# Weight buffers at alternating 64-byte offsets, and the later adaLN columns ordered behind a low part on VectorE, in a two-layer hybrid decoder trunk

## The chip, the cores and the metric

The kernel runs on one core of one Trainium2 chip, in one launch. The metric is the device time of that core in microseconds. Three runs of the kernel before gave 904.12, 908.38 and 950.62 us, with the median at 908.38 us. The execution that the profiler took, on which every row below rests, took 906.63 us; its span from the first to the last instruction is 904.9 us, so 1.7 us lie around the span.

## The reference, cut to what matters

Two layers work on x of 256 positions by 1024 features in float32. Each layer computes

```python
mod = c_act @ ada_w + ada_b                     # 1024 -> 3 x 1024: shift, scale, gate
h = rmsnorm(x, norm_g) * (1 + scale) + shift
z = h @ w_in                                    # 1024 -> 13312, for all three branches
ya = rg_lru(causal_dwconv(a_x)) * silu(a_g)     # branch A
yb = merged dilated window attention * silu(b_g)  # branch B: 3 groups x 8 heads x 64
yc = rmsnorm(gla_chunked(c_q, c_k, c_v)) * silu(c_g)  # branch C: 4 heads
merged = mg0 * (ya @ proj_a) + mg1 * (yb @ proj_b) + mg2 * (yc @ proj_c)
x = x + gate * (merged @ w_o)
```

The adaLN product `c_act @ ada_w` has one row only. The kernel treats it as 24 columns of 128 outputs a layer: shift and scale are the first 16 columns, the gate is the last 8.

## The kernel before, in words

All weights come from memory in a fixed stream of 288 units, 144 a layer (`layer_units`, line 39). The order in a layer is: q, k, v and b_g of the first head pair; then the head pairs and branch A mixed; mA (units 68 to 75) and pA (76 to 83), with the attention of the last head pair beside them; c0 to c3 (units 84 to 107); mC, pC, mB, pB and wo (units 108 to 143). In the second layer every number is 144 higher. There are two kinds of unit for what follows:

- **F and P units** (and b_g): the weight is the stationary operand, loaded 128 columns at a time, and 256 positions of the activations move past it. `mm_f` (lines 803 to 809) issues three matmuls for each of 8 slices of the contraction: high weight by high activation, high by low, low by high.
- **Streamed units** (kind "T" other than b_g): 128 positions of the activations are stationary and 384, 400 or 512 weight columns move (`mm_t`, lines 775 to 801), again three matmuls for each slice.

Each weight is split in two for float32r: ScalarE casts the loaded tile `raw` to the high part `whi` (line 232), and VectorE subtracts to get the low part `wlo` (line 233). `advance(i + 3)` does this for the unit three ahead of the one TensorE works on, so there are four buffers of `whi` and four of `wlo`, and six of `raw`. A buffer has 1040 floats, that is 4160 bytes, 64 more than a multiple of 256, so that buffers which lie one behind the other start 64 bytes further past a multiple of 256 each time. The kernel then lets a unit use the buffer from its start or from 64 bytes in (`o`, line 225). In the built program the four buffers of the high parts lie together, and those of the low parts lie together. With `o`, the weights of the units i = 0, 1, 2, 3 (modulo 4) start 64, 192, 192, 64 bytes past a multiple of 256 in F and P units, high and low alike, and 0, 0, 128, 128 in streamed units. The activations start at 0 (`hhi`, `hlo`, `mhi`, `mlo`) or at 128 (`yhi`, `ylo`).

The adaLN columns run in the same stream. A column is a 512 KB transfer into a `raw` buffer on SyncE's queue (line 208) and one custom reduction of 128x1024 on VectorE (`ada_tile`, line 334), with a small read of its accumulator behind it; every second one has a product of one column behind it (line 336). Sixteen columns of the first layer run at the start, ahead of the units they belong to (`START`). The other 32 stand one behind every third unit, from unit 68 of each layer on (`REST`): the first layer's gate and the second layer's shift and scale (24 columns, units 68 to 137), and in the second layer its gate (8 columns, units 212 to 233).

The program is written in this order, but a scheduler orders each engine's instructions by its own estimate of when they can start, unless `tc.issue_after` holds one behind another. Nothing holds the 32 later columns in the kernel before. Each engine then works strictly in its order: while VectorE waits for a column's transfer, the low parts and the evacuations behind it wait too.

Of the kernel before, what the change touches and what calls it, by code (L numbers as in the profile page):

```python
# [10 lines left out]
F32 = mybir.dt.float32  # L11
F32R = mybir.dt.float32r
I32 = mybir.dt.int32
AF = mybir.ActivationFunctionType
ALU = mybir.AluOpType
# [3 lines left out]
D, S, L, P = 1024, 256, 2, 128  # L19
# [53 lines left out]
def unit_elems(u):  # L73
    return {"T": 2 * u[4], "F": 1024, "P": 1024}[u[0]]
# [52 lines left out]
def hybrid_trunk(ctx: ExitStack, tc: tile.TileContext, ws, ada, vec, gates, a2, qkg, c_t, x_t, pos, inv, eye,  # L127
                 mask, tri, rst, out):
    nc = tc.nc
    V, A, G, T, SY = nc.vector, nc.scalar, nc.gpsimd, nc.tensor, nc.sync  # L130
# [10 lines left out]
    wts = ctx.enter_context(tc.tile_pool(name="wts", bufs=LEAD + 1))  # L141
# [42 lines left out]
    cur = {}  # L184


    raw_t, w_t = {}, {}
    at_item = [0, 0]
    early = {}

    def load_next():
        n = at_item[0]
        if n >= len(items):
            return
        at_item[0] += 1
        it = items[n]
        if it in early:
            raw_t[n] = early[it]
            cur["sy", "a", it[2]] = SY.dma_start(out=early[it], in_=ada[it[1], it[2]]).ins
            return load_next()  # L200
        if it[0] == "u":
            e = unit_elems(units[it[1]][1])
            o = offs[it[1]]
            t = wts.tile([P, e], F32, name="raw", tag="raw", bufs=NRAW)
            cur["sy", it[1]] = SY.dma_start(out=t, in_=ws[o:o + e * P].rearrange("(p n) -> p n", p=P)).ins
        else:
            t = wts.tile([P, D], F32, name="raw", tag="raw", bufs=NRAW)
            SY.dma_start(out=t, in_=ada[it[1], it[2]])
        raw_t[n] = t

    def advance(i):

        while at_item[1] < len(items):
            n = at_item[1]
            it = items[n]
            if it[0] == "u" and it[1] > i:
                return
            at_item[1] += 1
            r = raw_t.pop(n)
            if it[0] == "u":  # L220
                e = unit_elems(units[it[1]][1])


                streamed = units[it[1]][1][0] == "T" and units[it[1]][1][1] != "bg"
                o = 16 * ((it[1] % 2 == 0) != streamed)
                hi = wts.tile([P, D + 16], F32R, name="whi", tag="whi")[:, o:o + e]
                lo = wts.tile([P, D + 16], F32R, name="wlo", tag="wlo")[:, o:o + e]
                with ExitStack() as st:
                    if it[1] < 4:
                        st.enter_context(tc.issue_after(cur["ra"]))  # L230
                        st.enter_context(tc.issue_after(cur["rv"]))
                    A.copy(hi, r)  # L232
                    V.tensor_tensor(lo, r, hi.bitcast(F32), ALU.subtract)  # L233
                w_t[it[1]] = (hi, lo)
            else:
                ada_tile(it[1], it[2], r)
            load_next()


# [64 lines left out]
    def vcol(l, c, n=1):  # L304
        return vec_sb[:, l, c:c + n]
# [24 lines left out]
    def ada_tile(l, c, w):  # L330
        a, b = acc[:, l, c:c + 1], vec_sb[:, l, V_ADA + c:V_ADA + c + 1]
        j, i = (c // 2, c % 2) if c < 16 else (c - 16, 2)
        m = mod[:, l, i, j:j + 1]
        V.tensor_tensor_reduce(w, w, crow2, 1.0, b, ALU.mult, ALU.add, a if i == 0 else m)  # L334
        if i == 0:
            V.tensor_tensor(m, a, vcol(l, V_NG + j), ALU.mult)
        if l == 0 and i == 1:
            h_tile(0, j, cur["rstd"], cur["h"])
# [24 lines left out]
    def h_tile(l, j, rstd, h):  # L363
        hi, lo = h
        t = tmp()
        V.scalar_tensor_tensor(t, x_sb[:, j], mod[:, l, 0, j:j + 1], rstd, ALU.mult, ALU.mult)
        sh = mod[:, l, 1, j:j + 1]
        a = A.activation(hi[:, j], t, AF.Identity, bias=sh)  # L368
        v = V.scalar_tensor_tensor(lo[:, j], t, sh, hi[:, j].bitcast(F32), ALU.add, ALU.subtract)  # L369
        cur["h_last"] = (a.ins, v.ins)  # L370
# [443 lines left out]
    def layer(l, h, first_extra):  # L814
# [6 lines left out]
        for i in range(base, base + per_layer):  # L821
            kind, nm, p, kk, n = units[i][1]
            advance(4 * (i // 4) + 3 if i < 12 else i + LEAD)
            if i in first_extra:
                first_extra[i]()
# [255 lines left out]
```

## Time and profile before

| what | value |
|---|---|
| median of three runs | 908.38 us |
| profiled execution | 906.63 us, span 904.9 us |
| TensorE (PE) busy | 865.6 us, 96% |
| VectorE (DVE) busy | 671.9 us, 74% |
| ScalarE (ACT) busy | 531.8 us, 59% |
| GpSimd (POOL) busy | 179.1 us, 20% |
| mean granted TensorE clock | 0.987 of full speed |
| DMA | 170.16 MB, mean 188 GB/s |

The busy share of TensorE says that it has something in flight nearly always. Matmuls overlap in the records, so the time that one takes off the next is read from the starts of two that follow each other, not from the duration of one. The list of costly groups gives the number of matmuls of each kind; the list of waits says for whom an engine sat idle; and the table of windows compares stretches. A good comparison is inside this kernel: both layers do the same work from unit 68 on, except that 24 adaLN columns run there in the first layer and 8 in the second.

### The profile page before, as it was taken

To read this page: it belongs to the slowest core of one execution; us is meant where nothing else is said; L and a number is where in the kernel's file an instruction comes from. 1 tells how busy PE (TensorE), PEld (TensorE's weight loads), DVE (VectorE), ACT (ScalarE), POOL (GpSimd) and SP (SyncE) were. 2 spreads that over 40 slices of the span, in tenths; PEclk is the share of its full clock that TensorE was granted. 3 is DMA by queue.
4 is the path that set the end of the run, shared out by engine and by line. 5 is a ranking of instruction groups with operands and counts; after the bars stand their busy time and mean duration, and the time that the engine had idled before them with its cause. 6 is when DMAs were issued, how large, how long until landed. Compare 5 with 4: busy or idle time off the path is not lost.

```text
span 904.9 us, 16407 instructions
## 1 busy us (share of the span) xinstructions
PE 865.6 (96%) x6340; PEld 818.7 (90%) x6340; DVE 671.9 (74%) x1115; ACT 531.8 (59%) x897; POOL 179.1 (20%) x160
## 2 busy tenths in 40 slices
PE   3989999999999999999999999989999999999998
PEld 2978999999988888998989999979999988899998
DVE  6998899669667667656776788986896666656674
ACT  4376976686544554644454689666874545554451
POOL 0026365224000110100030525651430001000000
PEclk7999999999999999999999999999999999999999
DMA  8884456446756666676654644553567455455651
GB/s 334 309 290 138 146 174 193 141 134 195 248 184 197 205 212 201 212 236 205 224 168 148 191 146 144 176 194 117 184 205 239 163 189 166 148 173 187 191 167 47
DMA packets 52111, 170.16 MB, mean 188 GB/s; under 512 B 6240, under 2 KB 8160, under 8 KB 52032
## 3 DMA queue, kind: packets, MB, share of 16 engines
q1 hardware_dynamic: 51216, 167.04, 56.8%
q10 hardware_dynamic: 672, 1.87, 0.7%
q8 instruction: 50, 0.82, 0.4%
q0 software_dynamic: 144, 0.20, 0.2%
q14 instruction: 29, 0.24, 0.1%
HBM read 168.23 MB, written 1.05 MB: 187 GB/s over the span
## 4 chain that ended last, share of the span: by engine, by line
PE 51%; DVE 19%; DMA 12%; issue 8%; ACT 5%; POOL 4%; DVEq 0%; SPq 0%; ACTq 0%
DMA raw<-in_ada_dram 10%; PE mm L807 10%; PE mm L809 10%; PE mm L808 10%; DVE wlo L233 8%; PE mm L799 5%; PE mm L800 5%; PE mm L801 4%; POOL ss L570 2%; PE xps L177 1%; ACT whi L232 1%; DVE raw L334 1%; DVE rb L564 1%; DMA g_raw<-in_gates_dram 1%; DVE ra L562 1%
## 5 line engine op out<-in xcount | busy, mean ns | idle before, releaser
L233 DVE TENSOR_TENSOR wlo<-raw,whi 128x1024 fp32r<-128x1024 f32 (+2 forms) x288 | 335.3, 1171 | 84.5 <-ACT whi L232 83.1
L232 ACT CAST whi<-raw 128x1024 fp32r<-128x1024 f32 (+2 forms) x288 | 280.1, 976 | 185.2 <-PE mm L808 120.4
L807 PE MATMUL mm<-hhi,whi 128*128 128x256 f32 x768 | 217.1, 283 | 2.9 <-DVE rb L564 2.9
L809 PE MATMUL mm<-hhi,wlo 128*128 128x256 f32 x768 | 216.0, 282 | 3.5 <-DVE wlo L233 3.5
L808 PE MATMUL mm<-hlo,whi 128*128 128x256 f32 x768 | 215.4, 280 | 0.0
L799 PE MATMUL mm<-whi,hhi 128*128 128x384 f32 (+2 forms) x480 | 169.5, 358 | 7.2 <-ACT hhi L368 6.5
L800 PE MATMUL mm<-wlo,hhi 128*128 128x384 f32 (+2 forms) x480 | 171.3, 358 | 1.6 <-DVE wlo L233 1.4
L801 PE MATMUL mm<-whi,hlo 128*128 128x384 f32 (+2 forms) x480 | 167.6, 355 | 0.5 <-DVE hlo L369 0.5
L807 PEld LDWEIGHTS mm<-hhi,whi 128*128 128x128 f32 x768 | 146.0, 190 | 4.5 <-ACT tmp L857 2.9
L809 PEld LDWEIGHTS mm<-hhi,wlo 128*128 128x128 f32 x768 | 145.6, 190 | 4.7 <-DVE wlo L233 4.1
L808 PEld LDWEIGHTS mm<-hlo,whi 128*128 128x128 f32 x768 | 145.7, 190 | 0.3
L799 PEld LDWEIGHTS mm<-whi,hhi 128*128 128x128 f32 x480 | 92.9, 195 | 14.5 <-ACT hhi L368 7.5
L800 PEld LDWEIGHTS mm<-wlo,hhi 128*128 128x128 f32 x480 | 93.4, 195 | 9.1 <-DVE wlo L233 3.2
L334 DVE CUSTOM_DVE_ANT_0 raw<-raw,crow,vec_sb 128x1024 f32<-128x1024 f32 x38 | 48.7, 1283 | 70.2 <-DMA raw<-in_ada_dram 70.2
L801 PEld LDWEIGHTS mm<-whi,hlo 128*128 128x128 f32 x480 | 92.5, 194 | 6.7 <-DVE hlo L369 0.8
L807 PE MATMUL mm<-yhi,whi 128*128 128x256 f32 x320 | 89.9, 281 | 1.5 <-DVE mg L949 1.5
L808 PE MATMUL mm<-ylo,whi 128*128 128x256 f32 x320 | 89.4, 279 | 0.0
L809 PE MATMUL mm<-yhi,wlo 128*128 128x256 f32 x320 | 89.2, 279 | 0.0
L807 PEld LDWEIGHTS mm<-yhi,whi 128*128 128x128 f32 x320 | 60.4, 189 | 2.5 <-DVE mg L949 1.7
L809 PEld LDWEIGHTS mm<-yhi,wlo 128*128 128x128 f32 x320 | 60.1, 188 | 0.8 <-DVE mod L334 0.4
L808 PEld LDWEIGHTS mm<-ylo,whi 128*128 128x128 f32 x320 | 60.1, 188 | 0.0
L708 POOL TENSOR_TENSOR at_hl<-att_sb,at_hl 128x384 fp32r<-128x384 f32 x8 | 8.8, 1096 | 206.3 <-ACT at_hl L707 206.3
(236 smaller groups left out, 1409.2 us busy)
## 6 DMA issues: line engine op xcount, KB each, us to landing
raw<-in_ws_dram SPq DMA_DIRECT2D x192, 512.0 KB, 4.2
raw<-in_ws_dram SPq DMA_DIRECT2D x88, 384.0 KB, 3.1
raw<-in_ada_dram SPq DMA_DIRECT2D x38, 512.0 KB, 4.5
raw<-in_ws_dram SPq DMA_DIRECT2D x8, 400.0 KB, 4.6
g_raw<-in_gates_dram ACTq DMA_DIRECT2D x3, 512.0 KB, 4.5
x_sb<-in_x_t_dram SPq DMA_DIRECT2D x2, 512.0 KB, 6.6
ada_yhi<-in_ada_dram SPq DMA_DIRECT2D x2, 512.0 KB, 7.8
ada_ylo<-in_ada_dram SPq DMA_DIRECT2D x2, 512.0 KB, 9.0
```

The lines of the kernel that those rows point to most:

```text
L177: seen[0] = T.transpose(*a, **k).ins
L232: A.copy(hi, r)
L233: V.tensor_tensor(lo, r, hi.bitcast(F32), ALU.subtract)
L334: V.tensor_tensor_reduce(w, w, crow2, 1.0, b, ALU.mult, ALU.add, a if i == 0 else m)
L562: V.tensor_tensor(ra.rearrange("p (g s) d -> p g s d", g=3), z4, ctab[l][:, i, t].unsqueeze(2).to_broadcast(bc), ALU.mult)
L570: G.tensor_tensor(ss, ss, mhalf[:, 0:12].rearrange("p (a b) -> p a b", a=2), ALU.pow)
L799: T.matmul(o, ah, wh, start=(k == 0), stop=False)
L800: T.matmul(o, ah, wl, start=False, stop=False)
L801: T.matmul(o, al, wh, start=False, stop=(k == KT - 1))
L807: T.matmul(ps[:, 0:S], hi[:, a:b], xh[:, k], start=(k == 0), stop=False)
L808: T.matmul(ps[:, 0:S], hi[:, a:b], xl[:, k], start=False, stop=False)
L809: T.matmul(ps[:, 0:S], lo[:, a:b], xh[:, k], start=False, stop=(k == nk - 1))
```

## The change

Two things change in `advance`. The buffers get a tag each (`whi0` to `whi3`, `wlo0` to `wlo3`, one buffer a tag), in place of four under one tag, and the offset no longer depends on whether the unit is even. In the built program the buffers now lie in turn, a high one, a low one, a high one. With the new offsets the weights of an F or P unit start 64 bytes past a multiple of 256 when the unit's number is even and 192 when it is odd, high and low alike. In a streamed unit the high part starts at 0 and the low part at 128 when the unit's number is even, and the other way round when it is odd. And each of the 32 later columns is held behind the low part that was issued last before it in the program; the first 16 are left as they were.

```diff
     raw_t, w_t = {}, {}
+    early_cols = {(0, c) for c in range(16)}
     at_item = [0, 0]
...
                 streamed = units[it[1]][1][0] == "T" and units[it[1]][1][1] != "bg"
-                o = 16 * ((it[1] % 2 == 0) != streamed)
-                hi = wts.tile([P, D + 16], F32R, name="whi", tag="whi")[:, o:o + e]
-                lo = wts.tile([P, D + 16], F32R, name="wlo", tag="wlo")[:, o:o + e]
+                o, q = 16 * streamed, it[1] % 4
+                hi = wts.tile([P, D + 16], F32R, name="whi", tag=f"whi{q}", bufs=1)[:, 16 - o:16 - o + e]
+                lo = wts.tile([P, D + 16], F32R, name="wlo", tag=f"wlo{q}", bufs=1)[:, o:o + e]
...
-                    V.tensor_tensor(lo, r, hi.bitcast(F32), ALU.subtract)
+                    cur["lo"] = V.tensor_tensor(lo, r, hi.bitcast(F32), ALU.subtract).ins
                 w_t[it[1]] = (hi, lo)
+            elif it[1:] in early_cols:
+                ada_tile(it[1], it[2], r)
             else:
-                ada_tile(it[1], it[2], r)
+
+                with tc.issue_after(cur["lo"]):
+                    ada_tile(it[1], it[2], r)
             load_next()
```

Counted by low parts, the first of the 32 columns stood behind the low part of unit 64 on VectorE and now stands behind that of unit 68; those for units 125, 128, 131, 134 and 137 stood behind 121, 124, 127, 130 and 133. All now stand behind exactly the low part that the program writes ahead of them, three to five low parts later than before. GpSimd and SyncE keep their order; on TensorE a piece of attention or of branch C moves by a unit at some places.

VectorE around unit 124 of the first layer, where mB begins, before (L233 is the low part, L334 the column and its accumulator read, L336 the column's product, L642 the last part of the attention, L921 and L922 pC's evacuation):

```order
L233 TENSOR_TENSOR wlo<-raw,whi 128x1024
L921 SCALAR_TENSOR_TENSOR mg<-mg,mm 128x256
L922 TENSOR_TENSOR mrg<-mrg,mg 128x256
L233 TENSOR_TENSOR wlo<-raw,whi 128x1024
L642 SCALAR_TENSOR_TENSOR ylo<-sgb,yhi 128x1024
L334 ISA raw,mod<-raw,crow,vec_sb 128x1024
L334 ISA mod 128x1
L233 TENSOR_TENSOR wlo<-raw,whi 128x1024 x3
L334 ISA raw,acc<-raw,crow,vec_sb 128x1024
L334 ISA acc 128x1
L233 TENSOR_TENSOR wlo<-raw,whi 128x1024
```

The same place in the changed program, whose line numbers are 2 higher for the low part and 6 higher for the rest:

```order
L927 SCALAR_TENSOR_TENSOR mg<-mg,mm 128x256
L928 TENSOR_TENSOR mrg<-mrg,mg 128x256
L235 TENSOR_TENSOR wlo<-raw,whi 128x1024
L648 SCALAR_TENSOR_TENSOR ylo<-sgb,yhi 128x1024
L235 TENSOR_TENSOR wlo<-raw,whi 128x1024
L340 ISA raw,acc<-raw,crow,vec_sb 128x1024
L340 ISA acc 128x1
L342 TENSOR_TENSOR mod<-acc,vec_sb 128x1
L235 TENSOR_TENSOR wlo<-raw,whi 128x1024 x3
L340 ISA raw,mod<-raw,crow,vec_sb 128x1024
L340 ISA mod 128x1
```

The column that stood between the attention's last part and three low parts now has one of these low parts ahead of it, and it is the column of an earlier place in the stream. The other place is the attention of the last head pair, beside pA. Before (L608 and L611 are the softmax, L634 its result, L915 pA's evacuation):

```order
L634 TENSOR_TENSOR sgb<-xps,sgb 128x2x128
L915 SCALAR_TENSOR_TENSOR mrg<-mg,mm 128x256
L334 ISA raw,mod<-raw,crow,vec_sb 128x1024
L334 ISA mod 128x1
L233 TENSOR_TENSOR wlo<-raw,whi 128x1024
L608 ISA pr,st<-ps_s,m_sb 128x512
L608 ISA st 128x1
L608 ISA pr,st<-ps_s,m_sb 128x512
L608 ISA st 128x1
L611 RECIPROCAL st<-st 128x1
```

In the changed program:

```order
L614 ISA pr,st<-ps_s,m_sb 128x512
L614 ISA st 128x1
L614 ISA pr,st<-ps_s,m_sb 128x512
L614 ISA st 128x1
L617 RECIPROCAL st<-st 128x1
L921 SCALAR_TENSOR_TENSOR mrg<-mg,mm 128x256
L617 RECIPROCAL st<-st 128x1
L235 TENSOR_TENSOR wlo<-raw,whi 128x1024
L340 ISA raw,mod<-raw,crow,vec_sb 128x1024
L340 ISA mod 128x1
L921 SCALAR_TENSOR_TENSOR mrg<-mg,mm 128x256
```

The column that stood ahead of this softmax now stands behind it and behind a low part.

## Rows read from the trace of the kernel before

**Rows 1.** Waits of VectorE, whole span: engine line waited for, us in total, times, longest.

```profile
DVE wlo L233 <- ACT whi L232: 83.1, 84, 2.1
DVE raw L334 <- DMA raw<-in_ada_dram: 70.2, 28, 4.7
```

**Rows 2.** The same waits, first layer from unit 68 on.

```profile
DVE raw L334 <- DMA raw<-in_ada_dram: 59.9, 21, 4.7
```

**Rows 3.** Windows: window, us, PE PEld DVE ACT POOL busy (x), PEclk, DMA share, GB/s.

```profile
276.90:359.70 82.80, 81.28 (x514) 70.25 (x512) 58.80 (x115) 42.37 (x75) 6.20 (x9) 1.00 0.66 214
720.10:800.10 80.00, 80.00 (x512) 69.72 (x512) 51.35 (x92) 43.39 (x78) 7.37 (x10) 1.00 0.53 172
406.40:432.90 26.50, 24.34 (x195) 23.93 (x194) 17.55 (x24) 11.34 (x16) 0.00 (x0) 0.94 0.68 216
846.00:868.10 22.10, 22.10 (x194) 22.10 (x193) 11.79 (x11) 11.33 (x16) 0.00 (x0) 1.00 0.63 191
432.90:468.30 35.40, 33.77 (x290) 33.22 (x289) 27.54 (x46) 18.48 (x29) 8.14 (x6) 1.00 0.65 202
868.10:901.40 33.30, 33.30 (x290) 33.25 (x288) 21.67 (x40) 12.35 (x18) 0.00 (x0) 1.00 0.29 93
420.60:424.00 3.40, 3.40 (x16) 3.40 (x17) 2.11 (x2) 0.00 (x0) 0.00 (x0) 0.50 1.00 290
```

**Rows 4.** Timeline of VectorE around mB: start us, us, instruction [idle before <-releaser].

```profile
414.03 1.22 DVE L642 SCALAR_TENSOR_TENSOR ylo<-sgb,yhi 128x1024 fp32r<-128x1024 f32 x1
418.01 1.28 DVE L334 CUSTOM_DVE_ANT_0 raw<-raw,crow,vec_sb 128x1024 f32<-128x1024 f32 x1 [2.76 <-DMA raw<-in_ada_dram]
419.22 3.49 DVE L233 TENSOR_TENSOR wlo<-raw,whi 128x1024 fp32r<-128x1024 f32 x3
```

**Rows 5.** Waits of TensorE, whole span.

```profile
PE mm L809 <- DVE wlo L233: 3.5, 3, 1.8
PE xps L177 <- ACT pr L612: 2.3, 4, 1.0
PE mm L807 <- DVE mg L949: 1.5, 1, 1.5
PE xps L721 <- DVE g_hi L687: 0.9, 1, 0.9
```

**Rows 6.** Timeline of TensorE in pC, units 264 and 265: starts, duration.

```profile
837.39 0.28 PE L809 MATMUL mm<-yhi,wlo 128*128 128x256 f32 x1
...
837.74 0.28 PE L809 MATMUL mm<-yhi,wlo 128*128 128x256 f32 x1
...
838.08 0.28 PE L809 MATMUL mm<-yhi,wlo 128*128 128x256 f32 x1
...
838.42 0.28 PE L809 MATMUL mm<-yhi,wlo 128*128 128x256 f32 x1
```

**Rows 7.** Windows of TensorE alone, second layer: units 260 to 264, 265 to 267.

```profile
823.70:837.85 14.15, 14.15 (x122) 1.00 0.59 187
837.85:846.00 8.15, 8.15 (x74) 1.00 0.59 192
```

**Rows 8.** Groups: line, engine, operation, shapes, count, then busy us and mean ns.

```profile
L807 PE MATMUL mm<-hhi,whi 128*128 128x256 f32 x768 | 217.1, 283 | 2.9 <-DVE rb L564 2.9
L800 PE MATMUL mm<-wlo,hhi 128*128 128x384 f32 x320 | 109.3, 343 | 1.5 <-DVE wlo L233 1.4
L800 PE MATMUL mm<-wlo,hhi 128*128 128x512 f32 x128 | 50.8, 397 | 0.0
```

**Rows 9.** Timeline of TensorE, streamed units 86 (from 282.97) and 105 (from 349.49).

```profile
282.97 0.39 PE L799 MATMUL mm<-whi,hhi 128*128 128x512 f32 x1
...
285.76 0.40 PE L799 MATMUL mm<-whi,hhi 128*128 128x512 f32 x1
...
349.49 0.39 PE L799 MATMUL mm<-whi,hhi 128*128 128x512 f32 x1
...
352.21 0.40 PE L799 MATMUL mm<-whi,hhi 128*128 128x512 f32 x1
```

## The prediction

> **What bounds the kernel now.** I read the waits first, then windows of equal work, then the starts of single matmuls. TensorE is busy 96% of the span, so time goes only where it waits, or where a matmul takes more time than its neighbours of the same shape.
>
> VectorE's waits have one entry that the change aims at: it sat idle 70.2 us in 28 waits, up to 4.7 us long, for a column's transfer [rows 1]. Of this 59.9 us in 21 waits fall in the first layer from unit 68 on [rows 2]. Idle time of VectorE is harmless as such; the low parts have about three units of slack. The windows show where it is not harmless. The same stages of both layers stand there in pairs [rows 3], with the same number of matmuls (514 and 512, 195 and 194, 290 and 290): c0 to c3 took 82.80 and 80.00 us, mB took 26.50 and 22.10 us, pB with wo 35.40 and 33.30 us. The first of each pair is the first layer, with 24 columns from unit 68 on, and the second has 8, the last of them in c0. So the first layer loses 2.8, 4.4 and 2.1 us, together 9.3 us.
>
> The mechanism is seen best in mB. After the attention's last part, begun at 414.03 and 1.22 us long, VectorE had nothing ready at the head of its queue but a column whose transfer was not there; it waited 2.76 us, worked 1.28 us on it, and only then did three low parts in a row, 3.49 us [rows 4]. TensorE, out of low parts, waited 1.8 us, the longest of three such waits that come to 3.5 us [rows 5]. Then its granted clock read 0.50 from 420.60 to 424.00, the 1.2 GHz level, having been at 1.00 before the wait: 16 matmuls in 3.40 us [rows 3], or 213 ns each. That is the lower level's own price: at about 114 ns the 16 would take 1.8 us, so 1.6 us went there.
>
> **The second thing, the step of one matmul.** In pC of the second layer the same three matmuls repeat. From L809 to L809 it took 0.35 us up to 837.74, then 0.34 us and 0.34 us [rows 6]. Small, but it lasts: units 260 to 264 took 14.15 us for 120 matmuls, 117.9 ns each, and units 265 to 267 took 8.15 us for 72, 113.2 ns each [rows 7]. (The counts in the rows include those that hang over the window's edge.) Nothing waits in either stretch, the clock is 1.00 in both, and the matmuls are of one kind. The switch falls on the unit where the weight's place goes from 64 to 192 past a multiple of 256. There are 3648 such matmuls (each of three lines has 768 and 128 and 320; one group stands in [rows 8]). So there are two steps, 4.7 ns apart, and something that has to do with where the weights start moves TensorE from the slow one to the fast. In the streamed units the place shows directly: unit 86, which starts at 128, took 2.79 us for 12 matmuls, 232.5 ns each, and unit 105, which starts at 0, took 2.72 us, 226.7 ns each [rows 9].
>
> **The change part by part.**
>
> *The columns' order.* No instruction is added or removed. The 32 columns move behind three to five low parts, about 8 to 14 us at the 2.8 us that a unit takes (22.10 us for eight units, [rows 3]); they waited 2.5 us on the average and 4.7 us at most [rows 1], so their transfers will have landed. On SyncE's queue the column's transfer is where it was; its buffer comes free later, but the next load needs the buffers ahead of it first, which are released by the low parts that it now follows, so no load starts later. What is queued behind a column on VectorE now waits for 1.28 us of work [rows 4] and not for a transfer. I take the whole loss of mB, 4.4 us, and of pB with wo, 2.1 us, as given back: there the wait of TensorE stands right behind a column that waited (the 1.8 us for a low part, and 1.5 us for `mg`, [rows 5]). Two further waits, 1.0 us for a softmax and 0.9 us for `g_hi` [rows 5], have a column some instructions ahead of them; of these 1.9 us I take half, 0.9 us, since other work lies between. Sum: 4.4 + 2.1 + 0.9 = 7.4 us. Bounds: from below, the full 9.3 us with both of these waits, 11.2 us; from above, no gain but a new stall of the size of mB's, 4.4 us slower. I am nearer the gain because the two stages without columns run without any such stall.
>
> *F and P units.* In the fast step TensorE stays fast from unit to unit, whatever the weights' place; it returns to the slow one where the activations change between those at 0 and those at 128, or after other matmuls. It leaves the slow step at a unit where the weights' place changes: in mA, mC and mB, whose activations start at 0, from 192 to 64; in pA and pC, whose start at 128, from 64 to 192, as between the two windows of [rows 7]. Such a place came once in four units, and comes now once in two. I take it that a run of eight units turns fast one and a half units sooner on the average, at 24 x 4.7 ns = 0.11 us a unit; 14 runs in the two layers give 2.3 us. In c0 to c3 the pairs of F units had the right change in half the cases and now have it in none, which takes back 0.4 us for four units; and after a reset not every chance turns it: units 260 to 264 let one pass [rows 7]. I take 1.5 us. Bounds: about half of the 3648 matmuls are slow (the eight units of mB took 22.10 us for 192, 115.1 ns each, [rows 3], between the two steps), so all fast gives 8.6 us, and all slow loses 8.6 us.
>
> *Streamed units.* Half of them started at 128 and half at 0; now each has its high part at one and its low part at the other, so that two of three matmuls read the one. Even and odd units balance, and I take nothing. Bounds: 1536 matmuls (480 in each of three lines besides 32 whose results go elsewhere; two of the groups are in [rows 8]), half of them now on each side, by the 5.8 ns of [rows 9]: 4.5 us either way, and that is generous, since the ones of 384 columns differ less.
>
> The tags and the buffer count are as many as before, four and four, and cost nothing: each unit still takes the buffer that the unit four before it used.
>
> Sum against the profiled execution's 906.63 us: 906.6 - 7.4 - 1.5 = 897.7, so **898 us**. The median of the runs is 908.38 us, 1.7 us above the profiled execution; a run was at 904.12 us.
>
> **A rule against the addresses.** The step changed where the weights' place did, with nothing else changing [rows 6, 7]. The Trainium skill, SBUF — State Buffer, section "SBUF: two separate sides", says that TensorE's port waits on nobody, and that it reads its moving and its stationary operand over ports of its own; by that, where the weights start would not matter. This trace does not agree: 117.9 ns against 113.2 ns, and 232.5 against 226.7. By that rule the sum would be 906.6 - 7.4 = 899.2 us.
>
> **The rivals.**
>
> 1. *Forecast*, 898 us, and 893 to 903 where the terms together stay within 5 us of this sum: chance 0.55.
> 2. *The stalls come back behind something else.* With the columns out of the way the low parts are on time, but each column still takes 1.28 us out of VectorE at the same stages, and VectorE is busier there in the first layer (17.55 of 26.50 us against 11.79 of 22.10 us, [rows 3]). If mB and pB lose as much as before, only the 1.5 us remain: 905 us. Against it: 34% of VectorE is free there. Chance 0.2.
> 3. *All F and P steps turn fast*: 906.6 - 7.4 - 8.6 = 891 us. For it: the fast step, once there, lasts. Against: every run begins slow. Chance 0.1.
> 4. *Slower: the columns now stand on the attention's way.* Beside mA and pA a column stood ahead of the softmax and waited; now it stands behind a low part and ahead of evacuations and copies that TensorE's transposes wait for. That is 16 columns in both layers, 1.28 us each, 20.5 us at most. It outweighs the gains from 8.9 / 16 = 0.56 us a column on. At 0.7 us, half and a little, it costs 11.2 us: 897.7 + 11.2 = 909 us, slower than before. Against it: TensorE's waits for softmaxes come to 2.3 us in the whole kernel [rows 5]. Chance 0.1.
> 5. *The weights' place does nothing*, and the two steps come from elsewhere: 906.6 - 7.4 = 899 us. The switch between the two windows of [rows 7] with nothing else changed speaks against it. Chance 0.05. It is what the skill's rule above gives.
>
> That the change does not do what it says I leave out: the order of the built program and the buffers' places show both.
>
> **Range and chances.** The range goes from rival 3's 891 us, less 1 us for the columns' best case, to rival 4's 909 us, less 1: 890 to 908. Outside are the cases in which the bounds add up. A measurement of this kernel tells about 2% from no change, 18 us: below 890 us it is faster by that, above 926 us slower. The first needs both gains near their bounds, 906.6 - 11.2 - 8.6 = 886.8; I give it 0.06. The second needs nearly all of rival 4's price on top of no other gain; 0.02. Within 2%: 0.92.
>
> **What would show it.** In the profile of the changed kernel: VectorE's wait for columns falls from 70.2 us to under 10 us; mB of the first layer takes 22 to 23 us at a clock of 1.00, and pB with wo 33.5 us; the wait of L809 for `wlo` falls from 3.5 us to under 2 us. Units 260 to 267 turn fast at or before unit 263, so that pC takes 21.9 to 22.2 us where it took 14.15 + 8.15 us. Streamed units of 512 columns take 2.74 to 2.77 us all alike. I am wrong on the order if VectorE's wait goes and the first layer's stages keep their time; wrong on the place if pC of the second layer does not change, or if mixed starts make a streamed unit longer than 2.79 us.

## The result, and the profile after

The changed kernel took 892.51 us (median of 5 runs, 890.75 to 893.66) against 905.01 us for the kernel before in the same comparison. The ratio is 0.9846 with a 95% interval of 0.9824 to 0.9868: 1.5% less time, clear of no change and, as forecast, less than 2%. (The two medians alone give 0.986, inside the interval; a slow run of the kernel before, 950.62 us, is left out of the ratio.) The forecast was 898 us with a range of 890 to 908 us. The profiled execution took 892.51 us with a span of 890.7 us, 14.2 us below the span before.

VectorE's waits of the changed kernel come first (engine, line, waited for: us in total, times, longest). The three longest are:

```profile
DVE wlo L235 <- ACT whi L234: 107.0, 107, 2.1
DVE x_sb L935 <- PE mm L815: 14.8, 7, 3.5
DVE ro L581 <- POOL ss L576: 14.7, 11, 2.5
```

The entry for the columns, 70.2 us in 28 waits [rows 1], has no successor: L340 appears in no row of this view. What grew is the wait of the low part for the high part, from 83.1 to 107.0 us. That is a good sign. VectorE waits there for work of a unit that TensorE has yet to reach, so it is time by which VectorE is ahead. The group of L340 says the same as the waits: 38 reductions and no idle time in front of them.

```profile
L340 DVE CUSTOM_DVE_ANT_0 raw<-raw,crow,vec_sb 128x1024 f32<-128x1024 f32 x38 | 50.3, 1326 | 0.0
```

TensorE's waits of the changed kernel:

```profile
PE mm L805 <- ACT hhi L374: 6.5, 1, 6.5
PE xps L328 <- DVE diag L324: 4.6, 1, 4.6
...
PE mm L815 <- DVE wlo L235: 1.3, 1, 1.3
```

The wait for `wlo` fell from 3.5 us in three [rows 5] to 1.3 us in one, and this one is early in the program (64 us). The wait for the softmax (L177 for `pr`) fell from 2.3 us [rows 5] to 0.2 us, and those of [rows 5] for `mg` and `g_hi` have no row. Between 218 and 455 us, from unit 68 to the end of the first layer's wo, TensorE waits for nobody: the view lists no row for that stretch.

Windows of the changed kernel tell where the time came from (columns as in [rows 3]). First layer, then second, of pA, of c0 to c3, of mC, of mB, and of pB with wo:

```profile
245.92:275.19 29.27, 29.27 (x258) 27.61 (x257) 20.04 (x37) 16.00 (x25) 0.00 (x0) 1.00 0.54 180
677.12:706.40 29.28, 29.28 (x259) 27.62 (x257) 20.05 (x37) 16.00 (x25) 0.00 (x0) 1.00 0.54 181
275.19:355.07 79.88, 79.88 (x513) 69.70 (x512) 59.91 (x115) 42.45 (x76) 7.33 (x10) 1.00 0.65 215
706.40:786.50 80.10, 80.10 (x513) 69.74 (x512) 50.96 (x91) 42.23 (x76) 7.35 (x10) 1.00 0.53 172
355.07:378.38 23.31, 23.31 (x206) 23.30 (x205) 17.40 (x24) 14.08 (x26) 2.38 (x3) 1.00 0.75 246
786.50:809.94 23.44, 23.44 (x206) 23.43 (x205) 12.91 (x16) 13.39 (x25) 0.89 (x2) 1.00 0.56 180
400.47:422.44 21.97, 21.97 (x194) 21.97 (x193) 14.68 (x18) 11.32 (x16) 0.00 (x0) 1.00 0.76 262
832.02:854.00 21.98, 21.98 (x194) 21.98 (x193) 11.78 (x11) 11.32 (x16) 0.00 (x0) 1.00 0.63 192
422.40:455.50 33.10, 33.10 (x290) 33.10 (x290) 27.55 (x48) 18.50 (x29) 7.53 (x6) 1.00 0.63 199
854.00:887.08 33.08, 33.08 (x290) 33.03 (x288) 21.67 (x40) 12.36 (x18) 0.00 (x0) 1.00 0.29 93
```

Each stage now takes as long in the first layer as in the second, to within 0.2 us, although the first layer has 24 columns there and the second 8. The clock is 1.00 in all ten, the 2.4 GHz level: the half-clock stretch of [rows 3] is gone with the wait ahead of it. Three windows of the kernel before are needed beside those of [rows 3], which the prediction did not use: pA of the first layer, pA of the second, mC of the first.

```profile
245.41:276.87 31.46, 29.91 (x258) 27.58 (x257) 20.09 (x39) 17.32 (x29) 0.00 (x0) 1.00 0.51 168
689.65:720.05 30.40, 29.60 (x258) 27.59 (x257) 18.87 (x35) 16.55 (x28) 0.00 (x0) 1.00 0.52 170
359.70:384.06 24.36, 24.02 (x206) 23.66 (x205) 17.66 (x27) 14.55 (x29) 3.39 (x4) 1.00 0.66 199
```

| stage | before, us | after, us | gain, us | forecast for the order |
|---|---|---|---|---|
| pA, first layer | 31.46 | 29.27 | 2.2 | with the next three, 0.9 |
| pA, second layer | 30.40 | 29.28 | 1.1 | |
| c0 to c3, first layer | 82.80 | 79.88 | 2.9 | |
| mC, first layer | 24.36 | 23.31 | 1.0 | |
| mB, first layer | 26.50 | 21.97 | 4.5 | 4.4 |
| pB and wo, first layer | 35.40 | 33.10 | 2.3 | 2.1 |

The six gains come to 14.0 us, nearly the whole 14.2 us of the span. VectorE's timeline in mB, where a column had waited 2.76 us ahead of three low parts [rows 4], now reads (start us, us, instruction, idle before it):

```profile
410.01 1.23 DVE L235 TENSOR_TENSOR wlo<-raw,whi 128x1024 fp32r<-128x1024 f32 x1 [1.50 <-ACT whi L234]
412.73 1.22 DVE L235 TENSOR_TENSOR wlo<-raw,whi 128x1024 fp32r<-128x1024 f32 x1 [1.49 <-ACT whi L234]
413.87 1.28 DVE L340 CUSTOM_DVE_ANT_0 raw<-raw,crow,vec_sb 128x1024 f32<-128x1024 f32 x1
...
415.45 1.22 DVE L235 TENSOR_TENSOR wlo<-raw,whi 128x1024 fp32r<-128x1024 f32 x1 [0.29 <-ACT whi L234]
```

The column fits into the pause of 1.5 us between two low parts, and the next low part even has 0.29 us to spare.

### The profile page after: what moved, and what is told of

It is laid out like the page before. It is cut to its first block, busy times and chain, and to the rows that moved or that the text cites. A ratio compares the mean times of both kernels' runs of the same rounds, so it can differ in the third digit from the quotient of the medians.

```text
span 890.7 us, 16392 instructions
## 1 busy us (share of the span) xinstructions
PE 859.3 (96%) x6340; PEld 816.1 (92%) x6340; DVE 677.4 (76%) x1115; ACT 533.3 (60%) x897; POOL 179.4 (20%) x160
## 4 chain that ended last, share of the span: by engine, by line
PE 78%; DVE 10%; issue 4%; POOL 3%; ACT 2%; DMA 1%; SPq 0%; DVEq 0%; ACTq 0%
PE mm L813 15%; PE mm L815 15%; PE mm L814 15%; PE mm L807 7%; PE mm L806 7%; PE mm L805 7%; DVE wlo L235 3%; PE xps L177 2%; PE xps L173 2%; PE ps_s L173 2%; POOL ss L576 1%; DVE ra L568 1%; DVE rb L570 1%; DMA x_sb<-in_x_t_dram 1%; POOL ro L574 1%
## 5 line engine op out<-in xcount | busy, mean ns | idle before, releaser
L235 DVE TENSOR_TENSOR wlo<-raw,whi 128x1024 fp32r<-128x1024 f32 (+2 forms) x288 | 336.6, 1172 | 109.0 <-ACT whi L234 107.0
L340 DVE CUSTOM_DVE_ANT_0 raw<-raw,crow,vec_sb 128x1024 f32<-128x1024 f32 x38 | 50.3, 1326 | 0.0
```

Source lines behind the costliest of these rows:

```text
L235: cur["lo"] = V.tensor_tensor(lo, r, hi.bitcast(F32), ALU.subtract).ins
```

## The experiments

Each comparison has the kernel before on the same chip, and the ratios are to it. It took 906.81 us beside the order alone, the places alone, the last eight columns held and the activations moved to 0; 906.49 us beside the short columns and the three other kernels with the activations at 0; 907.69 us beside the repeated columns and the offset turned round. Spans are those of the one profiled execution of each kernel, and runs of one kernel differ by 0.5 to 6.6 us, so a difference of spans under 1 us says little by itself.

**The order alone, and the places alone.** The first kernel has the buffers of before and only this:

```diff
+    early_cols = {(0, c) for c in range(16)}
...
-                    V.tensor_tensor(lo, r, hi.bitcast(F32), ALU.subtract)
+                    cur["lo"] = V.tensor_tensor(lo, r, hi.bitcast(F32), ALU.subtract).ins
                 w_t[it[1]] = (hi, lo)
+            elif it[1:] in early_cols:
+                ada_tile(it[1], it[2], r)
             else:
-                ada_tile(it[1], it[2], r)
+                with tc.issue_after(cur["lo"]):
+                    ada_tile(it[1], it[2], r)
```

> The later columns held behind the low part as in the change, the buffers and offsets of the kernel before: every engine has the order of the changed kernel. Theory A (the order gives most of the gain: the stalls of TensorE behind a waiting column, and the slow clock after one, are gone in the whole first layer): 11 us faster than before, 894 us; VectorE's wait for columns near 0. Theory B (the order gives the 7.4 us forecast, and the weights' place the rest): 898 us.

It took 892.58 us (892.25 to 892.75), ratio 0.9844, interval 0.9824 to 0.9863, with a span of 891.0 us. That is the whole effect of the change (0.9846), as theory A has it. The second kernel is the changed one with the columns left free:

```diff
-                with tc.issue_after(cur["lo"]):
-                    ada_tile(it[1], it[2], r)
+                ada_tile(it[1], it[2], r)
```

> The alternating buffers and offsets of the change, the columns left free as before: every engine has the order of the kernel before. Theory A: 1.5 us faster than before, 903.5 us, with the stall and the slow clock at mB still there. Theory B: 5 us faster, 900 us. If the place does nothing: 905 us.

It took 906.27 us, ratio 0.9995 (0.9980 to 1.0010), span 907.0 us: nothing, where 1.5 or 5 us were expected. (The profiled execution, 908.80 us, was among the slowest of the twelve.) Its VectorE still waits for columns, and its TensorE for what stands behind them. VectorE's waits, whole span:

```profile
DVE raw L338 <- DMA raw<-in_ada_dram: 72.1, 28, 5.4
```

TensorE's, from 218 to 470 us:

```profile
PE mm L813 <- DVE wlo L235: 2.4, 3, 1.7
PE mm L811 <- DVE mg L953: 2.3, 1, 2.3
```

Its mB of the first layer:

```profile
408.93:434.37 25.44, 23.16 (x194) 22.48 (x193) 17.56 (x24) 11.32 (x16) 0.00 (x0) 1.00 0.71 220
```

The stall in mB is there, as theory A expected, but the slow clock is not: the granted clock is 1.00, the 2.4 GHz level, behind a longest wait of 1.7 us for a low part, where it read 0.50 behind 1.8 us in the kernel before. So the half-clock stretch is no fixed part of the loss. The order carries the result, and the places add nothing to it that these runs resolve.

**Only the last eight columns held.** As the first kernel, with `early_cols` so large that only the columns behind units 116 to 137 are held:

```diff
-    early_cols = {(0, c) for c in range(16)}
+    early_cols = {(l, c) for l in range(L) for c in range(24)} - {(1, c) for c in range(8, 16)}
```

> Buffers and offsets as before; only the last 8 of the 24 columns in the first layer (units 116 to 137, second layer's shift and scale from column 8 on) are held behind the low part, the other 24 later columns are free. Theory A, with the losses local to the stage in which a column waits: mB and pB with wo give 6.5 us, 898.5 us, and pA and c0 to c3 of the first layer stay as before. Rival (the stall comes back behind another wait while any columns wait upstream): under 2 us, 903 us or more.

It took 899.89 us, ratio 0.9924 (0.9905 to 0.9943). Its windows of pA and of mB in the first layer:

```profile
245.99:277.92 31.93, 30.08 (x258) 27.80 (x257) 19.86 (x39) 17.32 (x29) 0.00 (x0) 1.00 0.49 167
407.21:429.30 22.09, 22.09 (x195) 22.09 (x193) 14.70 (x18) 11.32 (x16) 0.00 (x0) 1.00 0.78 261
```

That is theory A's 898.5 us to within 1.4 us. mB has its full gain (22.09 us), and pA, whose columns are still free, has none (31.93 us). The loss belongs to the stage in which the column stands; no stage hands it on to the next.

**A column with its wait but nearly without its work.** The kernel before, columns free, where each of the 32 later columns reduces only 64 of 1024 elements. This leaves most of the adaLN product out of the computation.

```diff
+        n = D if (l, c) < (0, 16) else 64
-        V.tensor_tensor_reduce(w, w, crow2, 1.0, b, ALU.mult, ALU.add, a if i == 0 else m)
+        V.tensor_tensor_reduce(w[:, 0:n], w[:, 0:n], crow2[:, 0:n], 1.0, b, ALU.mult, ALU.add, a if i == 0 else m)
```

> The kernel before, but each of the 32 later columns reduces 64 of its 1024 elements (part of the adaLN product is left out); the transfers stay, and the columns stay free, ahead of low parts. Theory A (the loss is VectorE's wait for the transfer at the head of its queue): the stalls stay, 903 to 906 us, VectorE's wait for columns still over 60 us. Rival (the loss is the 1.28 us of work in front of the low parts, 32 times): the stalls go as with the order, 893 us.

It took 895.69 us, ratio 0.9880 (0.9863 to 0.9896), span 893.9 us. The group of L335 shows 302 ns a column in place of 1283 ns, and still 58.8 us of waiting:

```profile
L335 DVE CUSTOM_DVE_ANT_0 raw<-raw,crow,vec_sb 128x64 f32<-128x64 f32 x32 | 9.7, 302 | 58.8 <-DMA raw<-in_ada_dram 58.8
```

In the first layer from unit 68 on (218 to 459 us), its window, its waits for a column and its waits for `whi`:

```profile
218.00:459.00 241.00, 239.63 (x1882) 226.37 (x1880) 156.93 (x297) 130.54 (x215) 20.55 (x21) 1.00 0.69 219
DVE raw L335 <- DMA raw<-in_ada_dram: 45.0, 21, 4.5
DVE wlo L233 <- ACT whi L232: 24.3, 29, 2.0
```

This was a surprise: most of the waiting is there (45.0 us of 59.9 us [rows 2]), and most of the loss is not. So neither the wait alone nor the work alone is the cause as the expectation stated it. What is left is their sum: the columns still wait, but with 0.30 us of work behind the wait in place of 1.28 us.

**Work without a wait.** Three kernels test the sum from the other side. They have the order of the change and so no wait, and repeat each later column's reduction once, twice or three times, with the next low part held behind the last repeat (the added lines for once, beside those of the order; the other two have 2 and 3 for the 1):

```diff
+                    if "col" in cur:
+                        st.enter_context(tc.issue_after(cur["col"]))
+                    cur["lo"] = V.tensor_tensor(lo, r, hi.bitcast(F32), ALU.subtract).ins
...
+    again = sml.tile([P, 1], F32, name="again")
...
+        for _ in range(1 if (l, c) >= (0, 16) else 0):
+            cur["col"] = V.tensor_tensor_reduce(w, w, crow2, 1.0, b, ALU.mult, ALU.add, again).ins
```

> The order of e1_order_only, with each of the 32 later columns' reduction done twice in a row (the second result is dropped) and the next low part held behind it, so that 2.56 us of VectorE work without any wait for a transfer stand in front of it. Theory (the loss comes when what stands ahead of a low part exceeds the low parts' lead, which in mB is about 4.0 us of wait and work, 2.76 + 1.28): 2.56 us are under that, so 893 to 895 us, mB of the first layer 22 to 23 us. Rival (VectorE's share of work is what costs): 32 x 1.28 = 41 us more work show in TensorE, 897 us and more.

It took 896.85 us, ratio 0.9891 (0.9869 to 0.9913): at the edge between theory and rival. mB took 22.09 us, as without the repeats, and c0 to c3 took 79.95 us; the 4.1 us of span that it lost against the order alone are for the most part in mA of the two layers (1.7 and 1.9 us), beside the attention of the last head pair, where VectorE has most else to do.

> The same with three reductions in a row, 3.84 us ahead of the next low part, still without a wait for a transfer. Theory: at about the 4.0 us that mB had, so the loss comes back in part: 896 to 905 us, with TensorE's waits for wlo back in the first layer. Rival (only a wait for a transfer costs, through the loads that it holds up): 893 us.

It took 910.1 us, ratio 1.0025 (1.0007 to 1.0043): the whole loss is back, and more than I expected, without any wait for a transfer.

> The same with four reductions in a row, 5.12 us ahead of the next low part. Theory: beyond the lead at each of the 32 places, so slower than the kernel before: 906 to 925 us. Rival (only a wait for a transfer costs): 893 to 895 us, since VectorE has a fifth of its time free even then.

It took 937.04 us, ratio 1.0330 (1.0304 to 1.0355): slower than the theory's 906 to 925 us. The sign was right and the size was not. The reason is in VectorE's account for the first layer from unit 68 on. The window of the kernel before from 218 us to the end of the layer's stages:

```profile
218.00:470.00 252.00, 243.86 (x1884) 227.89 (x1883) 177.74 (x300) 130.20 (x216) 24.05 (x23) 0.99 0.66 211
```

VectorE's lead in the same stretch, that is its wait for `whi`:

```profile
DVE wlo L233 <- ACT whi L232: 7.1, 11, 1.2
```

The same stretch of the kernel with the columns three times, 93% busy with 234.81 of 251.50 us:

```profile
218.00:469.50 251.50, 243.34 (x1880) 227.95 (x1880) 234.81 (x396) 129.90 (x214) 25.80 (x22) 0.99 0.64 212
```

And its lead:

```profile
DVE wlo L236 <- ACT whi L233: 1.9, 4, 0.8
```

The changed kernel in its stretch:

```profile
218.00:457.00 239.00, 238.10 (x1885) 224.99 (x1883) 182.72 (x302) 132.12 (x216) 22.38 (x22) 1.00 0.68 224
```

Its lead:

```profile
DVE wlo L235 <- ACT whi L234: 28.7, 31, 2.1
```

The table has these and the other kernels, read from the same two views (all in us but the share):

| kernel | stretch, us | VectorE busy | blocked by a column | together | lead |
|---|---|---|---|---|---|
| after | 239.0 | 182.7 | 0 | 76% | 28.7 |
| short columns | 241.0 | 156.9 | 45.0 | 84% | 24.3 |
| columns twice | 240.5 | 208.1 | 0 | 87% | 14.7 |
| columns three times | 251.5 | 234.8 | 0 | 93% | 1.9 |
| before | 252.0 | 177.7 | 59.9 [rows 2] | 94% | 7.1 |
| columns four times | 283.0 | 269.3 | 0 | 95% | 0.8 |

The kernel before, with 177.7 us of work and 59.9 us of waiting, takes as long as one with 234.8 us of work and no waiting. A wait at the head of VectorE's queue fills VectorE just as work does, because nothing else can be done in it. Up to some 87% the stretch hardly grows, from 93% on it grows with VectorE. Four reductions are beyond that: three low parts and four reductions come to 3 x 1.24 + 4 x 1.28 = 8.8 us for each three units, where TensorE needs 3 x 2.76 = 8.3 us. By this account VectorE is there the slower of the two.

**The places, taken apart.** The fourth kernel of the first comparison moves the one kind of activation that starts at 128 (`yhi`, `ylo`) to 0, by allocating a small table later, and is else the changed kernel:

```diff
-    inv_sb = one.tile([P, 32], F32, name="inv_sb")
...
     rst_sb = one.tile([P, S], F32, name="rst_sb")
+    inv_sb = one.tile([P, 32], F32, name="inv_sb")
```

> The changed kernel with one 128-byte constant tile allocated later, so that the activations of pA, pC and pB start at a multiple of 256 as those of the other stages do. If the return to the slow matmul step where the activations change comes from their place (128 against 0), a fast step now lasts from mA, mC and mB on: about 3 us faster than the changed kernel, 889.5 us, pC of the second layer 21.8 us. If any other tile of activations brings the slow step back: as the changed kernel, 892.5 us.

889.37 us, ratio 0.9809 (0.9789 to 0.9829), as expected, and pC of the second layer took 21.76 us. The same with the streamed weights of q, k and v at 0 in every buffer (the added lines; they replace those for `hi` and `lo`):

```diff
+                oh, ol = (32 * (q % 2), 48 - 32 * (q % 2)) if streamed and e <= 800 else (16 - o, o)
+                hi = wts.tile([P, D + 16], F32R, name="whi", tag=f"whi{q}", bufs=1)[:, oh:oh + e]
+                lo = wts.tile([P, D + 16], F32R, name="wlo", tag=f"wlo{q}", bufs=1)[:, ol:ol + e]
```

> The changed kernel with the activations of pA, pC and pB at a multiple of 256, and now the weights of the q, k and v units (384 and 400 columns) at a multiple of 256 too, in every buffer. If the step of a streamed matmul goes by where its moving weights start (173 ns at 0, 176 to 177 at 128): about 500 matmuls of 1152 go to the short step, 1.5 us, 888 us. If it does not: 889.4 us.

889.72 us, ratio 0.9807 (0.9791 to 0.9823). No gain in time: a miss, although the slow steps of 384 columns went from 436 to 122 (table below). The order and the moved activations without the alternation, that is with the buffers of before:

> The order of the change and the activations at a multiple of 256, with the buffers and offsets of the kernel before (places 64, 192, 192, 64). If the place's alternation is worth little by itself, the activations give their 3 us here too: 889.5 us. If the alternation is what lets a slow step end, a slow stretch lasts up to four units and not two, and this is 1.5 us longer than with it: 891 us.

890.13 us, ratio 0.9815 (0.9801 to 0.9829), between the two expectations, and the time does not tell them apart. The counts do: F and P units have 1155 slow steps here and 1150 with the alternation (table below), so with the activations at 0 the alternation gives nothing. And the order, the activations at 0, q, k and v at 0, and all other weights at 64 in every buffer, so that nothing alternates (the added lines):

```diff
+                q = it[1] % 4
+                o, pad = 48 * (streamed and e <= 800), 16 * (q == 0)
+                hi = wts.tile([P, D + pad], F32R, name="whi", tag=f"whi{q}", bufs=1)[:, pad + o:pad + o + e]
+                lo = wts.tile([P, D + 48 * (q == 3)], F32R, name="wlo", tag=f"wlo{q}", bufs=1)[:, o:o + e]
```

> The changed kernel's order, activations at a multiple of 256, q, k and v weights at a multiple of 256, and the weights of all F and P units and of c0 to c3's streamed units 64 bytes past one in every buffer, without any alternation. If the place 64 by itself makes the fast step (after transposes the fast step came at 64 and the slow one at 192): nearly all F and P matmuls fast, 5 us less than the changed kernel with the activations at 0, 884 us. If the alternation is needed to leave the slow step: the runs that begin slow stay slow, 892 us or more.

887.66 us (887.24 to 888.40), ratio 0.9788 (0.9773 to 0.9804). It gained less than expected, and it is the fastest kernel of this study. The last one is the changed kernel with the offset turned round, so that F and P units start at 0 and 128 and streamed ones at 64 and 192:

```diff
-                o, q = 16 * streamed, it[1] % 4
+                o, q = 16 * (not streamed), it[1] % 4
```

> The changed kernel with the offset the other way round: F and P units at 0 and 128 in turn, streamed units at 64 and 192. Theory (the place sets the step, the stages hide it): more matmuls in the slow step, streamed ones of 384 and 512 columns nearly all slow (about 1000 more by 3 to 6 ns, 4 us), F units not known, so 894 to 900 us. Rival (the place does nothing in the sum): 892 to 893 us, as after and e1.

904.44 us, ratio 0.9972 (0.9957 to 0.9987), span 903.2 us. That is 12.5 us of span more than the changed kernel, beyond what was expected, with the same instructions and no wait of a new kind (TensorE's listed waits come to 29.6 us, against 27.6 us). The two kernels ran in different comparisons, where their ratios are 0.9972 and 0.9846, 1.3% apart, or 11 us. The streamed part of the expectation missed: 432 matmuls of 384 columns are slow, about as many as in the changed kernel (446), and not nearly all.

This offset changes two things. In an F or P unit the high part now starts at 0 and the low part at 128 or the other way round, while in the other kernels of the table both start at one place. No run separates the other places from the two parts being apart. The windows of pC in the second layer, eight units of 24 matmuls. The changed kernel, units 260 to 264 and units 265 to 267, as in [rows 7]:

```profile
809.94:823.87 13.93, 13.93 (x123) 13.93 (x122) 9.51 (x13) 5.53 (x6) 0.00 (x0) 1.00 0.60 190
823.87:832.02 8.15, 8.15 (x74) 8.15 (x73) 6.22 (x9) 3.15 (x3) 0.00 (x0) 1.00 0.58 194
```

With the offset turned round, all eight:

```profile
819.98:842.79 22.81, 22.81 (x194) 22.81 (x193) 15.71 (x22) 8.68 (x9) 0.00 (x0) 1.00 0.61 185
```

With the activations at 0, all eight:

```profile
807.97:829.73 21.76, 21.76 (x195) 21.76 (x193) 15.73 (x22) 8.69 (x9) 0.00 (x0) 1.00 0.62 196
```

Divided by 192 matmuls: 115.0 ns in the changed kernel (22.08 us in all), 118.8 ns with the offset turned round, 113.3 ns with the activations at 0. Nobody waits in any of them, and the clock is 1.00. Over the whole program, counted from the starts of the matmuls (a pitch is the time from one start to the next; of the F and P units 115 ns or less is called fast, up to 126 ns slow; with 512 columns over 228 to 245 ns is slow, with 384 over 174 to 182 ns; longer ones, around waits and at the lower clock, are left out):

| kernel | F and P, slow / fast | 512 columns, slow | 384 columns, slow | span, us |
|---|---|---|---|---|
| before | 1835 / 1880 | 227 | 421 | 904.9 |
| places alone | 1715 / 2011 | 262 | 467 | 907.0 |
| order alone | 1836 / 1910 | 216 | 428 | 891.0 |
| after | 1563 / 2183 | 258 | 446 | 890.7 |
| order, activations at 0 | 1155 / 2591 | 216 | 417 | 887.6 |
| after, activations at 0 | 1150 / 2597 | 270 | 436 | 887.6 |
| the same, q, k, v at 0 | 1077 / 2672 | 272 | 122 | 887.8 |
| all at 64 | 653 / 3094 | 273 | 133 | 886.3 |
| offset turned round | 3583 / 171 | 325 | 432 | 903.2 |

The mean of the F and P pitches counted here is 115.2 ns in the changed kernel and 118.7 ns with the offset turned round. Over some 3750 matmuls that is 13 us, the whole difference of the two.

## Why the prediction was right, and where it was not

**The mechanism of the order** held: VectorE's wait for columns is gone, mB went to 21.97 us and pB with wo to 33.10 us, where 22 to 23 us and 33.5 us were forecast, and the clock stayed at 1.00 there. The order alone gives 892.58 us.

**The size of the order's term was the step that failed.** It said 7.4 us; the span of the order alone is 13.9 us shorter. The 4.4 and the 2.1 us came as forecast (4.4 and 2.2 us with the order alone). What failed is "of these 1.9 us I take half": pA, c0 to c3 and mC gave 7.2 us where 0.9 us was taken, and even the bound of 11.2 us was too low. Two readings led there. First, the pairs of layers: pA was not compared, and in pA the pair could not show the loss, since the second layer has columns there too (30.40 us before, 29.28 us after). For c0 to c3 the pair did show 2.8 us [rows 3], and I took less because no long wait of TensorE stood next to it. Second, the sum went by the waits of TensorE that stand right behind a column. Small delays do not show there: c0 to c3 lost 2.9 us, while TensorE's two listed waits in that stretch came to 1.4 us. The view that would have told it is VectorE's account: 58.80 us busy [rows 3] and 23.1 us blocked by columns fill 81.9 of the 82.80 us, and the wait for `whi`, its lead, was 0.5 us there (VectorE's waits of the kernel before from 276.90 to 359.70 us):

```profile
DVE raw L334 <- DMA raw<-in_ada_dram: 23.1, 8, 3.8
DVE wlo L233 <- ACT whi L232: 0.5, 1, 0.5
```

**"34% of VectorE is free there"** was the argument against rival 2. It counted blocked time as free. In mB 17.55 us of work [rows 3] and its waits for columns left nothing of 26.50 us. The view gives 9.6 us for the three columns that begin there; 2.1 us of these lie ahead of the window, and 1.3 us of the next column's wait lie in it, so 8.9 us are blocked and 26.4 us filled. VectorE's waits for columns from 406.40 to 432.90 us:

```profile
DVE raw L334 <- DMA raw<-in_ada_dram: 9.6, 3, 4.1
```

The rival still did not come true, for the reason that the experiments show: without the waits VectorE has 24% left in the first layer, and 1.28 us a column fit in. They would not fit in three times.

**The term for F and P units** was 1.5 us, and its mechanism holds in part. With the columns' order the same in both, the changed places took the slow steps from 1836 to 1563, which at 117.9 - 113.4 = 4.5 ns is 1.2 us. In pC of the second layer the switch came at unit 263, as said (13.93 us for units 260 to 264 in place of 14.15 us [rows 7]). The term that failed here is the streamed units' nothing: 42 more of 512 columns and 18 more of 384 are slow, 0.3 us, and TensorE's listed waits rose by 0.5 us. Against the order alone, the change's span is only 0.3 us shorter, which is less than the runs of one kernel differ by. Streamed units 86 and 105, which took 2.79 and 2.72 us [rows 9], take 2.80 and 2.74 us in the changed kernel; the 2.74 to 2.77 us that I gave for all alike did not come, and unit 86 is over the 2.79 us that I named as a sign of being wrong on the place, if only by 0.01 us. The reading behind the term was too simple as well: in the kernel before all 16 streamed units of 512 columns that start at 128 have a median pitch of 230.5 to 233.5 ns, but of the 16 at 0 only ten have 227 ns, and six have 229 to 233 ns.

```profile
281.29:284.09 2.80, 2.80 (x15) 2.26 (x13) 1.82 (x8) 1.37 (x2) 0.00 (x0) 1.00 0.85 224
344.89:347.63 2.74, 2.74 (x13) 2.25 (x12) 2.65 (x4) 1.05 (x1) 0.00 (x0) 1.00 0.50 130
```

**The rivals.** Rival 3, all F and P steps fast, did not happen: 1563 remained slow; its 891 us was close to the time for another reason. Rival 4, columns on the attention's way, is refuted: pA became 2.2 and 1.1 us shorter, and TensorE's wait for the softmax fell from 2.3 us to 0.2 us. Rival 5, that the places do nothing, is right in the sum (0.9995 for the places alone) and wrong in what it says of the chip. By the rule of the Trainium skill, SBUF — State Buffer, section "SBUF: two separate sides", TensorE waits on nobody at its port, and the places would not matter. The trace disagrees more strongly than before: 118.8 ns against 113.3 ns in the same stage, and 12.5 us in the span by nothing but offsets of 64 bytes. That the change gained next to nothing by its places because it kept the same set, 64 and 192, and only changed the turn in which they come, fits the counts with the activations at 0 (1150 slow with the alternation, 1155 without), but no run tests it for the activations at 128.

In sum: 906.6 - 13.9 - 0.3 = 892.4 us, and 892.51 us was measured. The forecast was 5.5 us too high: 6.5 us too little for the order, 1.2 us too much for the places, and the rest is rounding.

## What to carry to other kernels

On an engine that works strictly in order, add the waits at the head of its queue for a transfer to its busy time before calling any of it free, stage by stage; its wait for the engine that feeds it is its lead, and a stage with no lead is bound by it even where the slower engine shows only small waits. A column of optional work belongs behind the work that is due, held there by hand when the scheduler hoists it. Before comparing a stage with its twin, ask whether the twin carries the same fault.

## What the runs showed of the hardware

The pitch of back-to-back matmuls at the 2.4 GHz level depends on where weights and activations start. With 256 columns it is 113.4 ns or 117.9 ns when the weights start at 64 or 192. It is 118.2 to 119.3 ns, unit by unit in pC, in the one kernel where one part of the weight starts at 0 and the other at 128; whether these places or the two parts being apart make that step is not shown. With 512 columns it is 226.7 or some 232 ns, and with 384 columns 173.3 or some 176.5 ns. The Trainium skill, TensorE: Matmul & The Clock Gate, section "Back-to-back issue gap", gives one gap for each number of columns: N / 2.4 + 2.5 ns at the higher clock for a matmul by itself, which makes an estimate of 109.2 ns for 256 and 215.8 ns for 512, and about 131 ns for 512 in a sustained stream. No pitch of these kernels at either number of columns is that short, and the trace has several steps for one number of columns.

The fast step, once there, lasts over units: in the changed kernel 64 of 64 changes of unit within the same activations kept it, where no wait and no other matmul came between. It was lost when the work went over to activations at another place, in 23 of 23 such changes in the kernels before and after. With `yhi` and `ylo` at 0 the same changes went between activations at one place, and 12 of 12 kept it. Of the 3.1 us of span that this move gave, the 413 slow steps fewer make 1.9 us; the rest is not traced.

After transposes (F and P matmuls with activations at 0, at least 12 in a row, in the table's kernels but the last and in that with the last eight columns held) the step was fast in 66 of 84 cases where the weights start at 64, and slow in 75 of 86 where they start at 192. That is a tendency and no rule: in the changed kernel a unit at 192 is fast from 607.6 us on. These kernels share most of their program, so these are not as many independent cases.

With all weights at 64 the slow steps fell from 1150 to 653, about 2.2 us, and those of 384 columns by 303, about 1 us; only 1.3 us of span came of it. TensorE's listed waits rose by 0.4 us, and the remainder is not traced. Why the step lasts, and what sets it, stays open: the runs tie it to the places and do not explain it. For the same reason the fastest kernel, 887.66 us, is a finding of these runs and not the end of what the places may give.
